# Layer 1's first weights and the kept down weights split behind layer 0's last gate tile, its down products ordered behind its last gate product, and modulation units moved to pairs 12 to 19

## The chip, the cores and the metric

The kernel runs on one core of one Trainium2 chip. A core has five engines with instruction queues of their own: TensorE (PE; the loading of its weights is listed as PEld), VectorE (DVE), ScalarE (ACT), GpSimd (POOL) and SyncE (SP). Transfers are issued from these queues and carried by 16 DMA engines that the core's queues share. The metric is the device time of one execution in microseconds (us). The kernel before takes 1612.67 us, the median of three runs (1612.62 to 1614.48).

## The reference

Two layers of a diffusion backbone work on 512 latent tokens and 256 context tokens of width 1024. Each layer has an attention block and a SwiGLU feed-forward block (FFN) of width 2816. What goes into each block is normalised, scaled and shifted, and what comes out is scaled by a gate. Those factors ("modulation vectors") come from the conditioning vector `c` for the latents, and from `c_ctx` for the context:

```
sh_a, sc_a, g_a, sh_f, sc_f, g_f = split(silu(c) @ mod_w[l] + mod_b[l], 6)
h_lat = h_lat + g_a * mixer(rms_norm(h_lat) * (1 + sc_a) + sh_a)
a     = rms_norm(h_lat) * (1 + sc_f) + sh_f
g, u  = split(a @ w_gate_up[l], 2)
h_lat = h_lat + g_f * ((silu(g) * u) @ w_down[l])
```

The context follows the same path in layer 0, with its own factors; in layer 1 it is only read. The output is the final normalisation of the latents.

## The kernel before, in words

Tokens lie along the free axis, so that a feature tile is 128 rows by 768 columns: `LATS` are the 512 latent columns, `CTXS` the 256 of the context. Products are taken in three matmuls (high by high, high by low, low by high part) of operands that were split into a rounded part and a remainder. ScalarE makes the rounded part (a cast, `S.copy`), VectorE the remainder (a subtraction). `load_w` (lines 313 to 320) loads a weight panel through the buffers "wr" (three of them) and splits it into "wh" and "wl"; `parts` (1328 to 1331) splits a tile into given buffers; `mm3` (322 to 333) issues the three products of a down or output tile.

Instructions on an engine are run in a fixed order. The tile framework works it out in advance, from a simulated timeline of its own, with waits on semaphores for data and for buffers. `behind(ins, *before)` adds an order between instructions on one engine, without a wait.

The FFN (`ffn`, line 1441 and on) works through the 22 pairs of gate and up tiles in chunks, in layer 0 `(0,4), (4,4), (8,4), (12,4), (16,3), (19,3)` as first pair and count. Here they are called chunks 0 to 5. Each pair (`Pair`) uses seven products of 12 matmuls on 384 columns (lines 1342 to 1344) in place of eight, with sums of operands made ahead. In `head`, product "11" goes to the bank z and "21" to x. In `body`, "T2" is added to z, "T3" opens y and "T1" is added to z. In `tail`, "22" is added to z and "T4" to y. Between these, ScalarE copies z (lines 1382, 1389, 1392), VectorE adds x to the copy (1383), ScalarE takes Silu of it (1384), and VectorE reads y (1393) before T4 may be added to it. After T4, lines 1397 to 1402 make the gate tile, which is cast (1329) and split (1330) into the operand of the down products. The tail of a pair is issued behind the head of the next one; the last pair of a chunk has its tail behind the loading of the chunk's first down weight.

After the pairs of a chunk come its down products: for each of eight tiles m, `down0` fetches the residual from DRAM (line 1197, POOL's queue), runs `mm3` on the latent and context columns, adds the result (1193) and stores the tile. In the program's order some of these products stand between the last products of the chunk's pairs. The last chunk of layer 0 uses `final0`: it goes through `output` (1212 on) with all latent tiles first and all context tiles after. Its weights come from `kept_w`, which loads each down weight once and keeps it for the second stream. `kept_w` for m=3, 4 and 5 also loads and splits panels 8, 9 and 0 of layer 1's input weights through "wr". Each latent tile is squared (ACT), and the squares are added by POOL and VectorE (366) to the sum whose product with ones (380) gives the norm of layer 1. The eight latent tiles are then stored in DRAM ("parked", line 1494) from ACT's queue, behind the square root of that norm.

The remaining modulation vectors are made in between. `bg(n)` takes n units from a generator. In this stage a unit (`mod_tile`, the branch for `late`) loads a 512 KB tile of `mod_w` into the single buffer "rope0" from POOL's queue (222) and reduces it on VectorE with the conditioning vector (227, a custom operation and a read of its accumulator). In layer 0's FFN there are 48 such loads; the first 16 tiles are reduced twice in their unit, once for the latents and once for the context, the other 32 once. `ffn` calls `bg(more(j))` after pair j, with

```
BG = ((0, 0, 0, 0, 0), (2, 3), (0, 0), (0, 0))
... lambda j: BG[1][j > 9] if j > 3 else j > 1
```

so that pairs 4 to 9 issue two units each and pairs 10 and on three each, until none is left. After `ffn` "rope0" takes the rotation tables of layer 1.

Of the kernel before, what the change touches and what calls it, by code (L numbers as in the profile page):

```python
# [10 lines left out]
F32R = mybir.dt.float32r  # L11
AF = mybir.ActivationFunctionType
ALU = mybir.AluOpType

P = 128
D = 1024
KT = D // P
# [10 lines left out]
CHUNKS = ((0, 4), (4, 4), (8, 4), (12, 4), (16, 3), (19, 3)), ((0, 3), (3, 3), (6, 4), (10, 4), (14, 4), (18, 4))  # L28
MLA_SCALE = 96.0 ** -0.5
LOWEST = -3.0e38  # L30
LATS = slice(0, NL)
CTXS = slice(NL, NT)
HT = NT // 2
TOK1, TOK2 = slice(0, HT), slice(HT, NT)
# [32 lines left out]
LOWER = 150  # L67
LOE = {(0, 2, 0): None, (0, 2, 1): None, (0, 5, 0): None, (0, 5, 1): 1, (1, 2, 0): None, (1, 2, 1): None, (1, 5, 0): None, (1, 5, 1): None}
PATTERN = ("fbsfbsfbbsfs",) * 3
BG = ((0, 0, 0, 0, 0), (2, 3), (0, 0), (0, 0))  # L70
FIRST = 2000
STEPS = ((2, 3, 4, 4), 5, 3)
HALVES = (slice(0, 256), slice(256, 512))
# [25 lines left out]
def hybrid_kernel(ctx: ExitStack, tc, I, out):  # L99
# [6 lines left out]
    def T(tag, shape, dt=F32):  # L106
        count[0] += 1
        if tag not in SIZES:
            return sb.tile(shape, dt, tag=tag, name=f"{tag}_{count[0]}", bufs=BUFS.get(tag, 1))
        n = int(np.prod(shape[1:]))  # L110
        t = sb.tile([P, SIZES[tag] // (2 if dt == mybir.dt.bfloat16 else 4)], dt, tag=tag, name=f"{tag}_{count[0]}",
                    bufs=BUFS[tag])[: shape[0], :n]
        if len(shape) == 3:
            t = t.rearrange("p (a b) -> p a b", a=shape[1])
        return t

    def B(dt=F32, tag="b"):
        return T(tag, [P, NT], dt)
# [22 lines left out]
    def behind(ins, *before):  # L141

        for x in before:
            tc.add_manual_dep(ins.ins, x.ins.name, mybir.DependencyInfo(mybir.DependencyClass.NoSync,
                              mybir.DependencyReason.DATA), reason="products in one run")
        return ins
# [37 lines left out]
    dense, tile, late, first = [True], [-9], [], {}  # L184
# [128 lines left out]
    def load_w(src, kt, m, eng=None, tag=None, after=()):  # L313

        r = T("wr", [P, kt * m])
        dma(r, src)
        h, lo = (B(F32R, tag)[:, : kt * m] if tag else T(x, [P, kt * m], F32R) for x in ("wh", "wl"))
        behind(S.copy(h, r), *after[:1])  # L318
        behind((G if eng else V).tensor_tensor(lo, r, f(h), op=ALU.subtract), *after[1:])  # L319
        return tuple(x.rearrange("p (k m) -> p k m", k=kt) for x in (h, lo))  # L320

    def mm3(outs, w, mov, first=True, last=True):

        wh, wl = w
        n = len(mov)
        begin = None
        for o, c in outs:
            for k, (mh, ml) in enumerate(mov):
                ins = PE.matmul(o, wh[:, k], mh[:, c], start=first and k == 0, stop=False)  # L329
                begin = begin or ins  # L330
                PE.matmul(o, wh[:, k], ml[:, c], start=False, stop=False)  # L331
                PE.matmul(o, wl[:, k], mh[:, c], start=False, stop=last and k == n - 1)  # L332
        return begin
# [5 lines left out]
    def PQ():  # L339
        return PS("d")  # L340

    outs = [0, None]

    def PO():

# [23 lines left out]
    marks = {}  # L369
# [383 lines left out]
    r = B(tag="nb")  # L753
# [120 lines left out]
    root, diag = first_norm(acc, LATS)  # L874
# [6 lines left out]
    for c in range(4):  # L881
# [5 lines left out]
        sums = []  # L887
# [24 lines left out]
    def beside(gen):  # L912
        side_work.append(gen)
        return gen
# [56 lines left out]
    rope0 = T("rope0", [P, 2, NL])  # L971
# [180 lines left out]
    def mla_jobs():  # L1152
        phase[0], lower[0] = 1, LOWER
        rate[0] = STEPS[1], BG[0][4]
        ready.append(latent_operands(1))
# [22 lines left out]

    H = []
    for k in range(KT):  # L1180
        t = B()
        dma(t, I["xn"][k])
        H.append(t)
    O += [in_rows(o, (B(F32R, "st"), B(F32R, "st"))) for o in OM]

    def add_residual(m, o, l, comp, v, c, dst=None, base=None):
        base = base or H[m]
        if c is TOK2:
            for x, v in pieces(c):
                ins = add_residual(m, o[:, x.start - HT : x.stop - HT], l, comp, v, x, dst, base)  # L1190
            return ins
        g = mod(l, comp, v, m)
        return V.scalar_tensor_tensor((dst or base)[:, c], o, g, base[:, c], op0=ALU.mult, op1=ALU.add)
# [3 lines left out]
        G.dma_start(t[:, c], home[m][:, c])  # L1197
        return t

    ahead, soon = {}, []  # L1200

    def kept_w(src, m):

        if 2 < m < 6:
            soon.append(load_w(I["w_in1"][(8, 9, 0)[m - 3]], KT, P))
        if m in ahead:
            return ahead[m]
        r, t = T("wr", [P, 384]), T("nb", [P, NT], F32R) if m < 2 else B(F32R, "st")
        dma(r, src(m))
        return tuple(x.rearrange("p (k m) -> p k m", k=3) for x in parts(r, t[:, :384], t[:, 384:]))  # L1210

    def output(src, mov, l, comp, streams, norm, units, dst=None, keep=False, base=None, wait=0):

        rest, kept, done = iter(()), [], []
        for i, (c, v) in enumerate(streams):
# [4 lines left out]
            for m in range(KT):  # L1220
# [9 lines left out]
                if c is TOK1:  # L1230
                    G.dma_start(home[m], H[m])
                norm.add(m, c)
# [93 lines left out]
        return Norm(src, use, G if l else None, (0, 4, 1, 5, 2, 6, 3, 7)), ops, sums  # L1326

    def parts(t, h, lo, after=()):
        S.copy(h, t)
        behind(V.tensor_tensor(lo, t, f(h), op=ALU.subtract), *after)  # L1330
        return h, lo

    norm, ops, sums = combined(H, 0, 3, TOK1, TOK2)
    output(lambda m: I["w_out0"][m], O, 0, 2, ((TOK2, 0), (TOK1, 0)), norm, BG[2])


    def product(o, w, x, first=False):

        for k in range(4):
            wh, wl = (y[:, k * P : k * P + P] for y in w)  # L1340
            xh, xl = x[k]
            PE.matmul(o, wh, xh, start=first and k == 0, stop=False, skip_group_check=not first)  # L1342
            PE.matmul(o, wh, xl, start=False, stop=False, skip_group_check=not first)  # L1343
            PE.matmul(o, wl, xh, start=False, stop=k == 3, skip_group_check=not first)  # L1344

    class Pair:

# [47 lines left out]
        def tail(self):  # L1395
            product(self.z, self.s4, self.ops["22"])
            S.activation(self.s[:, self.c2], self.z, AF.Silu)
            product(self.y, self.u2, self.ops["T4"])
            V.tensor_tensor(self.t[:, self.c1], self.y, self.t[:, self.c1], op=ALU.add)
            for c in (self.c2, self.c1) if self.w > NX else (slice(0, 2 * self.w),):  # L1400
                V.tensor_tensor(self.s[:, c], self.s[:, c], self.t[:, c], op=ALU.mult)
                parts(self.s[:, c], *(x[:, c] for x in self.dst))
# [38 lines left out]
    def ffn(l, ops, sums, cs, tags, own, more, down, final):  # L1441

        for ci, (k0, kc) in enumerate(CHUNKS[l]):
            hs, last = [], None
            for j in range(k0, k0 + kc):
                if j == 0:
                    hs.extend(first_pairs(l, ops, cs, tags, own))
                    if l == 0:
                        bg(1)
                    sums()  # L1450
                elif j >= DIRECT[l]:
                    p = Pair(l, j, ops, cs, tags[j - k0], (near_done[3],) if j == DIRECT[l] and l == 0 else ())
                    p.head()
                    if last:
                        last.tail()
                    p.body()
                    hs.append(p.dst)
                    last = p
                bg(more(j))
            src = lambda m: I["w_dn"][l, m, :, k0 * P : (k0 + kc) * P]  # L1460
            ahead.clear()
            ahead[0] = load_w(src(0), kc, P) if l or ci < len(CHUNKS[l]) - 1 else kept_w(src, 0)
            if last:
                last.tail()
            if ci < len(CHUNKS[l]) - 1:
                for m in range(KT):
                    down(m, lambda: ahead.get(m) or load_w(src(m), kc, P), hs)
            else:
                final(src, hs)

    new = []
    norm1, A = modulated(new, 1, 0, G, LATS)
# [9 lines left out]
    def final0(src, hs):  # L1482
        new.extend(B() for _ in range(KT))
        old = [fetched(m, slice(0, NT), "b") for m in range(KT)]
        output(src, hs, 0, 5, STREAMS0, norm1, BG[3], new, kept_w, lambda m, c: old[m], 1)

    ffn(0, ops, sums, (TOK1, TOK2), ("st", "st", "b", "b"), norm.marks[0], lambda j: BG[1][j > 9] if j > 3 else j > 1, down0, final0)
    H = new


    parked = []
    for k in range(KT):
        t = dr.tile([P, NL], F32, name=f"parked{k}")
        behind(S.dma_start(t, H[k][:, LATS]), norm1.marks[0]["root"])
        parked.append(t)
    rope1 = T("rope0", [P, 2, NL])
    dma(rope1, I["rope1"])
# [30 lines left out]
    for t0, n in ((0, 4), (4, 2)):  # L1528
        o = PS("t")
# [40 lines left out]
    H = []  # L1570
    for k in range(KT):
        t = B()
# [3 lines left out]
    norm, ops, sums = combined(H, 1, 3, *HALVES)  # L1576
# [124 lines left out]
```

## Time and profile before

| what | value |
|---|---|
| median of three runs | 1612.67 us (1612.62 to 1614.48) |
| the profiled execution's own time | 1610.99 us |
| its span in the profile | 1609.1 us |
| TensorE busy | 1541.6 us, 96% of the span |
| VectorE busy | 1183.8 us, 74% |
| ScalarE busy | 799.0 us, 50% |
| POOL busy | 298.6 us, 19% |
| layer 0: first product of chunk 3, chunk 4, chunk 5 | 766.40, 860.17, 930.99 us |
| layer 0: the norm's product with ones | 1003.50 us |

A row of the timeline gives the start in us, the duration in us, the engine, the line of the kernel, the operation, output from inputs, sizes and, in brackets, the idle time of the engine just before it with what ended it. Matmuls are pipelined, so their durations overlap: their price is the distance between starts. The page's fifth part lists groups of instructions: busy time and mean duration in ns, then the engine's idle time before them and what ended most of it.

### The profile page before, as it was taken

To read this page: it belongs to the slowest core of one execution; us is meant where nothing else is said; L and a number is where in the kernel's file an instruction comes from. 1 tells how busy PE (TensorE), PEld (TensorE's weight loads), DVE (VectorE), ACT (ScalarE), POOL (GpSimd) and SP (SyncE) were. 2 spreads that over 40 slices of the span, in tenths; PEclk is the share of its full clock that TensorE was granted. 3 is DMA by queue.
4 is the path that set the end of the run, shared out by engine and by line. 5 is a ranking of instruction groups with operands and counts; after the bars stand their busy time and mean duration, and the time that the engine had idled before them with its cause. 6 is when DMAs were issued, how large, how long until landed. Compare 5 with 4: busy or idle time off the path is not lost. (4 is left out here: it accounts for less than half of the span.)

```text
span 1609.1 us, 26559 instructions
## 1 busy us (share of the span) xinstructions
PE 1541.6 (96%) x9990; PEld 1371.1 (85%) x9990; DVE 1183.8 (74%) x2380; ACT 799.0 (50%) x1616; POOL 298.6 (19%) x324
## 2 busy tenths in 40 slices
PE   5989989999999999999999998999999999999997
PEld 3777867776899999998989896877779899899997
DVE  4773878668577678796867686779877688687685
ACT  4452587677365334342423244467756544354453
POOL 0231734230011111102021212384002000000002
PEclk9999999999999999999999998999999999999999
DMA  9634232102453455536456655132005133223322
GB/s 330 226 115 157 70 122 78 40 9 74 165 200 102 152 198 182 203 121 261 170 195 214 235 206 222 66 93 77 2 17 187 38 114 126 86 99 125 87 93 84
DMA packets 76536, 214.91 MB, mean 134 GB/s; under 512 B 10196, under 2 KB 17752, under 8 KB 76408
## 3 DMA queue, kind: packets, MB, share of 16 engines
q1 hardware_dynamic: 57432, 141.67, 26.4%
q0 software_dynamic: 16240, 68.30, 12.1%
q10 hardware_dynamic: 2736, 3.26, 0.6%
q8 instruction: 78, 1.28, 0.3%
q14 instruction: 50, 0.41, 0.1%
HBM read 186.97 MB, written 23.07 MB: 131 GB/s over the span
## 5 line engine op out<-in xcount | busy, mean ns | idle before, releaser
L318 ACT CAST wh<-wr 128x1024 fp32r<-128x1024 f32 (+2 forms) x148 | 114.8, 789 | 203.8 <-DMA wr<-in_w_dn_dram 35.4
L319 DVE TENSOR_TENSOR wl<-wr,wh 128x1024 fp32r<-128x1024 f32 (+2 forms) x145 | 135.1, 938 | 84.6 <-ACT wh L318 80.7
L553 ACT ACTIVATE p<-p,sm 128x512 f32<-128x512 f32 (+3 forms) x144 | 105.0, 730 | 32.4 <-DVE sm L557 30.5
L366 POOL TENSOR_TENSOR p<-p,p 128x256 f32<-128x256 f32 (+1 forms) x33 | 31.7, 960 | 468.5 <-PE psd L332 340.2
L1342 PE MATMUL pss<-b,wh 128*128 128x384 f32 (+1 forms) x344 | 107.0, 312 | 0.6 <-ACT b L355 0.6
L1343 PE MATMUL pss<-b,wh 128*128 128x384 f32 (+1 forms) x344 | 107.2, 312 | 0.1
L227 DVE CUSTOM_DVE_ANT_0 p<-rope,cond 128x1024 bf16<-128x1024 f32 x64 | 77.3, 1224 | 40.8 <-DMA rope<-in_mod_w_dram 40.5
L1344 PE MATMUL pss<-b,wl 128*128 128x384 f32 (+1 forms) x344 | 106.1, 312 | 0.0
L331 PE MATMUL psd<-b,wh 128*128 128x512 f32 (+3 forms) x256 | 88.2, 345 | 0.0
L329 PE MATMUL psd<-b,wh 128*128 128x512 f32 (+3 forms) x216 | 78.4, 363 | 2.9 <-ACT b L493 2.5
L547 PE MATMUL pso<-ph,b 128*64 128x256 f32 (+1 forms) x384 | 77.6, 360 | 2.1 <-DVE ph L492 2.1
L332 PE MATMUL psd<-b,wl 128*128 128x512 f32 (+3 forms) x216 | 77.1, 357 | 0.1
L547 PE MATMUL pso<-pl,b 128*64 128x256 f32 (+1 forms) x384 | 76.9, 359 | 0.2 <-DVE pl L492 0.2
L222 POOL DMA_DIRECT2D rope<-in_mod_w_dram x48 | 25.5, 531 | 244.1 <-DVE mod L227 229.3
L1344 PE MATMUL pst<-b,wl 128*128 128x384 f32 (+1 forms) x224 | 69.9, 312 | 0.0
L1343 PE MATMUL pst<-b,wh 128*128 128x384 f32 (+1 forms) x224 | 69.8, 312 | 0.0
L1342 PE MATMUL pst<-b,wh 128*128 128x384 f32 (+1 forms) x224 | 69.8, 312 | 0.0
L329 PE MATMUL pss<-st,wh 128*128 128x512 f32 (+2 forms) x200 | 68.2, 341 | 1.3 <-ACT st L1144 0.9
L331 PE MATMUL pss<-b,wh 128*128 128x256 f32 (+3 forms) x211 | 68.5, 325 | 0.1
L332 PE MATMUL pss<-st,wl 128*128 128x512 f32 (+2 forms) x200 | 68.0, 341 | 0.1
L1342 PEld LDWEIGHTS pss<-b,wh 128*128 128x128 f32 x344 | 65.2, 190 | 1.1 <-ACT b L355 0.9
L1343 PEld LDWEIGHTS pss<-b,wh 128*128 128x128 f32 x344 | 65.3, 190 | 0.9 <-DVE b L356 0.7
(674 smaller groups left out, 5423.8 us busy)
## 6 DMA issues: line engine op xcount, KB each, us to landing
wr<-in_w_gu_dram SPq DMA_DIRECT2D x88, 512.0 KB, 4.0
rope<-in_mod_w_dram POOLq DMA_DIRECT2D x48, 512.0 KB, 3.8
wr<-in_w_out_dram SPq DMA_DIRECT2D x32, 512.0 KB, 3.7
wr<-in_w_dn_dram SPq DMA_DIRECT2D x64, 256.0 KB, 2.8
p<-home POOLq DMA_DIRECT2D x40, 384.0 KB, 5.6
home<-p POOLq DMA_DIRECT2D x40, 384.0 KB, 5.0
wr<-in_w_in_dram SPq DMA_DIRECT2D x21, 512.0 KB, 3.9
nb<-in_nb_dram SPq DMA_DIRECT2D x16, 384.0 KB, 3.0
```

Of the source, the lines that this page charges most:

```text
L227: V.tensor_tensor_reduce(out=T("p", [P, D], mybir.dt.bfloat16), in0=w, in1=cond[:, v, :], op0=ALU.mult, op1=ALU.add, scale=1.0, scalar=0.0 ...
L318: behind(S.copy(h, r), *after[:1])
L319: behind((G if eng else V).tensor_tensor(lo, r, f(h), op=ALU.subtract), *after[1:])
L329: ins = PE.matmul(o, wh[:, k], mh[:, c], start=first and k == 0, stop=False)
L331: PE.matmul(o, wh[:, k], ml[:, c], start=False, stop=False)
L332: PE.matmul(o, wl[:, k], mh[:, c], start=False, stop=last and k == n - 1)
L366: marks["add"] = (eng or V).tensor_tensor(acc[:, :n], acc[:, :n], t[:, :n], op=ALU.add)
L547: ins = PE.matmul(o[64 * i : 64 * i + 64, c], v(kt), t, start=n == 0, stop=n == len(moving[i]) - 1)
L553: S.activation(p[:, c], p[:, c], AF.Exp, bias=nm, scale=-1.0, accum_out=dn)
L1342: PE.matmul(o, wh, xh, start=first and k == 0, stop=False, skip_group_check=not first)
L1343: PE.matmul(o, wh, xl, start=False, stop=False, skip_group_check=not first)
L1344: PE.matmul(o, wl, xh, start=False, stop=k == 3, skip_group_check=not first)
```

## The change

Five edits.

1. `BG[1]` goes from (2, 3) to (2, 4) and its switch from j > 9 to j > 11. Pairs 4 to 11 issue two units each and pairs 12 to 19 four each; the total of 48 loads stays.
2. `mm3` puts the first product of each output `behind` the list `tail_end`, which holds the last T4 product of the chunk's last pair. It applies to each `mm3` with `first`, in the chunks of both layers; the list is emptied after layer 0's `ffn`, and filled again in layer 1.
3. In the last chunk of layer 0 the kept weights m=0 and 1 are loaded and split ahead of the last tail. From m=2 on their casts and splits are put behind the cast and the split of the last gate tile (`split_behind`, `tails`).
4. Panels 8, 9 and 0 of layer 1's input weights are loaded after kept weights 3, 5 and 7 (before: ahead of 3, 4 and 5), panels 8 and 9 through "rope0" instead of "wr", and are split behind the same tile.
5. The parked stores are issued from POOL's queue, without the order behind the square root.

```diff
-BG = ((0, 0, 0, 0, 0), (2, 3), (0, 0), (0, 0))
+BG = ((0, 0, 0, 0, 0), (2, 4), (0, 0), (0, 0))
...
+        hold = tail_end if first else ()
         for o, c in outs:
             for k, (mh, ml) in enumerate(mov):
                 ins = PE.matmul(o, wh[:, k], mh[:, c], start=first and k == 0, stop=False)
+                if k == 0:
+                    behind(ins, *hold)
...
-    ahead, soon = {}, []
+    ahead, soon, tails = {}, [], []
+
+    def split_behind(r, h, lo):
+
+        behind(S.copy(h, r), *tails[:1])
+        behind(V.tensor_tensor(lo, r, f(h), op=ALU.subtract), *tails[1:])
+        return h, lo
 
     def kept_w(src, m):
 
-        if 2 < m < 6:
-            soon.append(load_w(I["w_in1"][(8, 9, 0)[m - 3]], KT, P))
         if m in ahead:
             return ahead[m]
         r, t = T("wr", [P, 384]), T("nb", [P, NT], F32R) if m < 2 else B(F32R, "st")
         dma(r, src(m))
-        return tuple(x.rearrange("p (k m) -> p k m", k=3) for x in parts(r, t[:, :384], t[:, 384:]))
+        w = split_behind(r, t[:, :384], t[:, 384:])
+        if m in (3, 5, 7):
+            r = T("wr" if m == 7 else "rope0", [P, D])
+            dma(r, I["w_in1"][{3: 8, 5: 9, 7: 0}[m]])
+            soon.append(tuple(x.rearrange("p (k m) -> p k m", k=KT) for x in split_behind(r, *(T(x, [P, D], F32R) for x in ("wh", "wl")))))
+        return tuple(x.rearrange("p (k m) -> p k m", k=3) for x in w)
...
     def parts(t, h, lo, after=()):
-        S.copy(h, t)
-        behind(V.tensor_tensor(lo, t, f(h), op=ALU.subtract), *after)
+        marks["cast"] = S.copy(h, t)
+        marks["split"] = behind(V.tensor_tensor(lo, t, f(h), op=ALU.subtract), *after)
         return h, lo
...
-            product(self.y, self.u2, self.ops["T4"])
+            self.end = product(self.y, self.u2, self.ops["T4"])
...
-            ahead[0] = load_w(src(0), kc, P) if l or ci < len(CHUNKS[l]) - 1 else kept_w(src, 0)
+            tails.clear()
+            if l or ci < len(CHUNKS[l]) - 1:
+                ahead[0] = load_w(src(0), kc, P)
+            else:
+                ahead.update({m: kept_w(src, m) for m in range(2)})
             if last:
                 last.tail()
+                tails[:] = [marks["cast"], marks["split"]]
+                tail_end[:] = [last.end]
...
-    ffn(0, ops, sums, (TOK1, TOK2), ("st", "st", "b", "b"), norm.marks[0], lambda j: BG[1][j > 9] if j > 3 else j > 1, down0, final0)
+    ffn(0, ops, sums, (TOK1, TOK2), ("st", "st", "b", "b"), norm.marks[0], lambda j: BG[1][j > 11] if j > 3 else j > 1, down0, final0)
     H = new
+    tail_end.clear()
...
-        behind(S.dma_start(t, H[k][:, LATS]), norm1.marks[0]["root"])
+        G.dma_start(t, H[k][:, LATS])
```

(`product` in the changed kernel returns its last matmul.)

More of the change, by code (lines that the diff above doesn't have):

```diff
@@ L340, in PQ @@
         return PS("d")
-    outs = [0, None]
+    outs, tail_end = [0, None], []
     def PO():
@@ L1343, in product @@
             PE.matmul(o, wh, xl, start=False, stop=False, skip_group_check=not first)
-            PE.matmul(o, wl, xh, start=False, stop=k == 3, skip_group_check=not first)
+            ins = PE.matmul(o, wl, xh, start=False, stop=k == 3, skip_group_check=not first)
+        return ins
     class Pair:
```

## The prediction

> **What bounds the kernel now.** I read the page's head first, to find the engine that sets the time; then the costliest groups, for the work that the change moves; then the tables by stage, because a share of the whole span says nothing about one chunk; then the timelines of the chunks that the change touches.
>
> ```profile
> span 1609.1 us, 26559 instructions
> PE 1541.6 (96%) x9990; PEld 1371.1 (85%) x9990; DVE 1183.8 (74%) x2380; ACT 799.0 (50%) x1616; POOL 298.6 (19%) x324
> ...
> L227 DVE CUSTOM_DVE_ANT_0 p<-rope,cond 128x1024 bf16<-128x1024 f32 x64 | 77.3, 1224 | 40.8 <-DMA rope<-in_mod_w_dram 40.5
> ...
> L222 POOL DMA_DIRECT2D rope<-in_mod_w_dram x48 | 25.5, 531 | 244.1 <-DVE mod L227 229.3
> ```
>
> TensorE is busy for 96% of the span, so a change wins only by closing one of its few gaps, and loses whatever it opens. The two groups below it are one modulation unit: POOL (L222) loads a 512 KB tile, and VectorE (L227) reduces it. POOL's idle time in front of L222 is 229.3 us, nearly all of it ended by L227: each load waits for the read before it, since "rope0" is a single buffer. VectorE in turn waits for the load, 40.5 us in all. The units are a closed chain.
>
> The two stages that receive the moved units, columns as time range, length, busy time and instructions of PE, PEld, DVE, ACT, POOL, granted clock, DMA share and GB/s:
>
> ```profile
> 772.00:836.00 64.00, 63.10 (x365) 61.56 (x364) 46.47 (x81) 23.30 (x45) 9.01 (x17) 1.00 0.47 158
> 866.00:913.00 47.00, 46.05 (x265) 44.47 (x263) 33.37 (x59) 16.45 (x33) 8.12 (x16) 1.00 0.46 155
> ```
>
> There PE lacks 0.90 of 64 and 0.95 of 47 us, at full clock. The chain is hidden today.
>
> **Price of a unit.** One turn of the chain (start, duration, engine, line), then starts in chunks 3 (pairs 12 to 15) and 4 (pairs 16 to 18):
>
> ```profile
> rope<-in_mod_w_dram POOLq DMA_DIRECT2D x48, 512.0 KB, 3.8
> ```
> ```profile
> 960.85 1.22 DVE L227 CUSTOM_DVE_ANT_0 p<-rope,cond 128x1024 bf16<-128x1024 f32 x1 [0.31 <-DMA rope<-in_mod_w_dram]
> ...
> 962.38 0.53 POOL L222 DMA_DIRECT2D rope<-in_mod_w_dram  x1 [4.86 <-DVE mod L227]
> ...
> 966.14 1.23 DVE L227 CUSTOM_DVE_ANT_0 p<-rope,cond 128x1024 bf16<-128x1024 f32 x1 [3.59 <-DMA rope<-in_mod_w_dram]
> ```
> ```profile
> 772.75 1.22 DVE L227 CUSTOM_DVE_ANT_0 p<-rope,cond 128x1024 bf16<-128x1024 f32 x1
> ...
> 789.45 1.23 DVE L227 CUSTOM_DVE_ANT_0 p<-rope,cond 128x1024 bf16<-128x1024 f32 x1 [1.05 <-DMA rope<-in_mod_w_dram]
> ...
> 794.57 1.23 DVE L227 CUSTOM_DVE_ANT_0 p<-rope,cond 128x1024 bf16<-128x1024 f32 x1 [0.68 <-DMA rope<-in_mod_w_dram]
> ...
> 805.94 1.22 DVE L227 CUSTOM_DVE_ANT_0 p<-rope,cond 128x1024 bf16<-128x1024 f32 x1
> ...
> 822.64 1.23 DVE L227 CUSTOM_DVE_ANT_0 p<-rope,cond 128x1024 bf16<-128x1024 f32 x1 [1.10 <-DMA rope<-in_mod_w_dram]
> ...
> 824.55 0.56 DVE L1393 TENSOR_TENSOR p<-pss,p 128x384 f32<-128x384 f32 x1 [0.20 <-ACT p L1392]
> ...
> 833.42 1.23 DVE L227 CUSTOM_DVE_ANT_0 p<-rope,cond 128x1024 bf16<-128x1024 f32 x1 [2.58 <-DMA rope<-in_mod_w_dram]
> ...
> 834.57 0.55 DVE L1399 TENSOR_TENSOR p<-pss,p 128x384 f32<-128x384 f32 x1
> ...
> 866.76 1.22 DVE L227 CUSTOM_DVE_ANT_0 p<-rope,cond 128x1024 bf16<-128x1024 f32 x1
> ...
> 909.89 1.23 DVE L227 CUSTOM_DVE_ANT_0 p<-rope,cond 128x1024 bf16<-128x1024 f32 x1 [1.82 <-DMA rope<-in_mod_w_dram]
> ```
>
> From read to issue 1.53 us, from issue to the next read 3.76: 5.29 us a unit. In chunk 3, 805.94 is the seventh unit and 833.42 the twelfth: 27.48/5 = 5.50 each. In chunk 4 the ninth comes 43.13 us after the first: 5.39. The shortest interval I found is 5.12 (789.45 to 794.57). VectorE works in a fixed order, so whatever stands behind a unit waits for that chain.
>
> The Trainium skill, "DMA: Bandwidth & Descriptors", section "Anatomy of one DMA — SWDGE (gpsimd) path", gives about 2.0 us plus bytes over 436 GB/s; by it 524,288 bytes would take an estimated 3.2 us, the turn 4.7, and the sum below would come out near 1627. This case's 3.8 us disagrees, and the measurement decides.
>
> PE's work is priced from these rows:
>
> ```profile
> 766.04 0.28 PE L329 MATMUL pst<-b,wh 128*128 128x256 f32 x1
> ...
> 766.40 0.34 PE L1342 MATMUL pss<-b,wh 128*128 128x384 f32 x1
> ...
> 814.38 0.33 PE L1342 MATMUL psd<-st,ph 128*128 128x384 f32 x1
> ...
> 816.46 0.39 PE L329 MATMUL psd<-st,wh 128*128 128x512 f32 x1
> ...
> 860.17 0.34 PE L1342 MATMUL pss<-b,wh 128*128 128x384 f32 x1
> ...
> 930.99 0.34 PE L1342 MATMUL pss<-b,wh 128*128 128x384 f32 x1
> ...
> 970.61 0.45 PE L1342 MATMUL pst<-st,wh 128*128 128x384 f32 x1 [0.57 <-ACT p L1389]
> ...
> 986.55 0.47 PE L329 MATMUL psd<-st,st 128*128 128x512 f32 x1 [1.96 <-DVE p L1399]
> ...
> 991.00 0.79 PE L329 MATMUL pst<-b,nb 128*128 128x512 f32 x1 [2.00 <-ACT b L1329]
> ...
> 997.24 0.39 PE L329 MATMUL pst<-st,st 128*128 128x512 f32 x1
> ...
> 999.28 0.28 PE L329 MATMUL psd<-st,nb 128*128 128x256 f32 x1
> ...
> 1003.50 0.87 PE L380 MATMUL pss<-ones,p 128*128 128x1 f32 x6 [2.98 <-DVE p L366]
> ```
>
> A gate/up product is 12 matmuls: 814.38 to 816.46, 2.08 us; a pair has seven, 14.6 us. Down products: nine of 512 columns take 2.04 (997.24 to 999.28), 0.227 each; three of 256 take 0.36, 0.12 each.
>
> **Term 1, chunk 3: +19.** Four pairs now carry 16 units, not 12. A pair's four units need 4 × 5.4 = 21.6 us, while PE spends 14.6 on it. In the changed program's VectorE order the x read of pair 15 (L1383 of before) stands behind unit 12, its y read (L1393) behind unit 13, its gate tile behind unit 14 and the first down residual behind unit 16. Before, the y read follows unit 10 (822.64, then 824.55) and the gate tile unit 12 (833.42, then 834.57). Unit 12 falls at about 833.4 again, since the chain starts with 772.75 and turns no faster. After it come the unit (1.23), the x read (0.55, as L1399's row), and on ScalarE the Silu, a weight cast and the z copy (three at about 0.5): T1 of pair 15 starts near 836.8. By pure work PE is there 25 products after 766.40, at 818.5, with the earlier gates of pair 14 at 822 to 824. It then idles some 12 us. Before, down products were mixed in at that place (816.46 is one); now each first down product is ordered behind the last T4, so nothing fills. T1 and 22 (4.2) and T4 (behind unit 13, 838.9 plus 1.8, and behind 22) end at 843.7. Eight down tiles of 12 × (0.227 + 0.12) are 33.3 us: the chunk ends near 877.0, not 860.17, +16.8. An idle of that length also brings the lower clock:
>
> ```profile
> 987.00:994.00 7.00, 5.00 (x13) 3.46 (x12) 2.13 (x5) 1.44 (x3) 0.00 (x0) 0.51 1.02 404
> ...
> 1004.00:1008.00 4.00, 4.00 (x22) 4.00 (x23) 1.35 (x3) 0.68 (x2) 0.00 (x0) 0.57 0.61 223
> ```
>
> Behind waits of 2 to 3 us (986.55, 991.00, 1003.50) the clock was 0.51 to 0.57 for 4 to 7 us, which costs half of that, 2 to 3.4. I take +19 (ends +16.8 and +20.2).
>
> The Trainium skill, "TensorE: Matmul & The Clock Gate", section "Part 1: The HAM clock gate", puts the half clock behind an idle window of about 3.4 us. By that the 0.57 us waits below cost no clock and these stalls do; the trace shows it already after 2 us.
>
> **Term 2, chunk 4: +13.4.** With s its first product: the first unit comes at s + 6.59 (866.76 against 860.17), unit 8 at s + 44.3, unit 10 at s + 55.1. Pair 18's x read stands behind unit 8, so T1 starts at s + 47.6, where PE is at s + 37.5 (18 products); its y read is behind unit 10, so T4 runs from s + 56.9 to 59.0. Eight tiles of 9 × 0.347 (25.0) and a 0.3 us switch end at s + 84.2, against 70.82 (930.99 less 860.17). Ends: +10 if the first units start 3 us earlier, +16.8 with a full dip of the clock.
>
> **Term 3, chunk 5 with the last output: -7.3.** Today 930.99 to 1003.50, 72.51 us, holds the waits 0.57, 1.96, 2.00 and 2.98 and the half clock. Changed: 252 matmuls × 0.1735 (43.7, plus 0.8 waits), 72 × 0.227 (16.4), nine of 256 (1.1), and 3.2 for residual, square and sums behind the last product, as between 1000.09 and 1003.50 in these rows:
>
> ```profile
> 1000.09 0.74 DVE L1193 SCALAR_TENSOR_TENSOR b<-pst,mod,b 128x512 f32<-128x512 f32 x1
> ...
> 1002.75 0.69 DVE L366 TENSOR_TENSOR p<-p,p 128x512 f32<-128x512 f32 x1
> ```
>
> That is 65.2. The kept weights m=0 and 1 are split before the gate tile, the rest behind it, so the waits on L1399 and L1329 go. The four units left there and the loads of panels 8, 9, 0 issue earlier and lie beside products. Two things are uncovered: panels 8 and 9 pass through "rope0" one after the other on SP's queue, with weight m=7 behind them (0 to +3.8, a landing); and the eight parked stores now stand in POOL's queue between its sums, seven of 0.53 us ahead of the third sum (0 to +3.7). I count both at 0, with under 1 us to spare. So the gain lies between 7.3 and nothing.
>
> **Term 4, held down products elsewhere: +4.6.** In chunks 0, 1, 2 and the five last tails of layer 1 nothing fills the wait between T2 and T1 for the z copy any more; it is 0.57 where the trace shows it unfilled (970.61). Eight times 0.57; ends 0 and +4.6, nearer the upper, since it is the same pair of products. Emptying pairs 4 to 11 of no unit, and giving chunk 2 two fewer, is worth nothing: those pairs hide them.
>
> **Sum.** 19 + 13.4 - 7.3 + 4.6 = +29.7. The profiled execution's own time is 1610.99, 1.7 below the median of 1612.67: 1640.7, forecast 1640.
>
> **Rivals.** A, the other side: the chain stays hidden. Unit 12 plus 3.4 would have to come before 818.5, so the turn may be no longer than (818.5 - 3.4 - 772.75)/11 = 3.85 us, below the 5.12 seen and hardly above the landing alone. For it: PE lost only 0.90 us in this stage. Then terms 1 and 2 vanish: 1611.0 - 7.3 + 2.3 (half of term 4) = 1606, faster. B, the same with all of term 4 and 3 us of term 3 lost: 1611.3, no change. C, milder: the turn is 4.7 us, as if issues overlapped reads; unit 12 falls 8 us earlier, chunk 4's tenth unit 6: 1640 - 7 - 6 = 1627. D, dearer: both stalls with the full dip, and term 3 given back by parked stores or panel loads: 1640.7 + 1.2 + 3.4 + 5 = 1650. Against D: the margins, though thin; for it, the DMA share of 1.02 in 987 to 994.
>
> **How the numbers follow.** Forecast 0.64, A 0.05, B 0.03, C 0.11, D 0.17. The range 1622 to 1652 takes in the forecast, C and most of D and leaves out A and B. Changes under 0.2% (3.2 us) can't be told from none here: faster 0.05 (A), same 0.03 (B), slower 0.92.
>
> **What would show it.** Right: L227 in chunks 3 and 4 back to back at 5.3 to 5.5 us; PE idle of 8 to 12 us ended by VectorE or ScalarE shortly ahead of the first down product of each; clock below 1 behind it; chunk 5 some 7 us shorter, without waits on L1399 and L1329; 0.57 us waits at the other tails. Wrong: a turn under 4.5 us, or x and y reads of pairs 15 and 18 that do not stand behind their units.

## The result and the profile after

The changed kernel takes 1642.64 us (median of five runs, 1641.59 to 1642.75), the kernel before, run beside it, 1613.51 us: a ratio of 1.0183, with a 95% interval of 1.0170 to 1.0196. It is slower by 29 us, where 1640 us was forecast. The profiled spans differ by 1639.8 - 1609.1 = 30.7 us, and that is what the parts below divide up.

The head of the changed kernel's page, and its row for a unit's reduction:

```profile
span 1639.8 us, 26564 instructions
...
PE 1551.4 (95%) x9990; PEld 1379.8 (84%) x9990; DVE 1187.1 (72%) x2380; ACT 799.7 (49%) x1616; POOL 303.3 (18%) x332
...
L227 DVE CUSTOM_DVE_ANT_0 p<-rope,cond 128x1024 bf16<-128x1024 f32 x64 | 77.2, 1223 | 46.4 <-DMA rope<-in_mod_w_dram 46.2
```

Nothing of this names the cause: TensorE's busy time grew by 9.8 us for the same 9990 matmuls, the other engines' by 4.7 us or less, and VectorE's wait for tiles grew from 40.5 to 46.2 us only. The stages tell it. The tables of windows, with the columns of the prediction, cut at the first products of chunks 3, 4 and 5 and at the norm's product; the kernel before:

```profile
766.40:860.17 93.77, 92.71 (x530) 87.73 (x529) 68.34 (x118) 32.79 (x60) 14.95 (x28) 1.00 0.58 202
860.17:930.99 70.82, 69.82 (x398) 65.90 (x397) 51.02 (x90) 23.95 (x46) 13.35 (x25) 1.00 0.61 217
930.99:1003.50 72.51, 64.75 (x336) 59.47 (x334) 55.34 (x94) 32.58 (x57) 13.22 (x20) 0.95 0.59 209
```

and the changed kernel:

```profile
766.44:877.15 110.71, 97.04 (x530) 90.60 (x529) 73.39 (x125) 32.81 (x60) 17.09 (x32) 0.95 0.53 183
877.15:962.33 85.18, 75.04 (x398) 69.86 (x397) 51.53 (x90) 23.54 (x44) 14.44 (x27) 0.90 0.54 190
962.33:1030.75 68.42, 62.13 (x336) 57.88 (x334) 54.24 (x88) 31.93 (x58) 15.22 (x24) 0.99 0.60 216
```

At the start of chunk 3 the two stand 0.04 us apart, which hides two differences: the changed kernel began layer 0's FFN 1.66 us sooner (513.25 against 514.91), in a stretch that the change doesn't touch, and its chunks 0 to 2 are longer by 0.47, 0.93 and 0.30, 1.70 in all. Chunk 3 is longer by 16.94 us, chunk 4 by 14.36, chunk 5 shorter by 4.09; what follows the norm's product is longer by 609.05 - 605.60 = 3.45. The same matmuls are spread over more time: in chunk 3 PE lacks 13.7 us, in place of 1.1.

The stall itself, in VectorE's timeline of the changed kernel (L1396 is the read of x, L1406 that of y):

```profile
771.34 1.22 DVE L227 CUSTOM_DVE_ANT_0 p<-rope,cond 128x1024 bf16<-128x1024 f32 x1
...
826.28 1.23 DVE L227 CUSTOM_DVE_ANT_0 p<-rope,cond 128x1024 bf16<-128x1024 f32 x1 [1.33 <-DMA rope<-in_mod_w_dram]
...
831.51 1.23 DVE L227 CUSTOM_DVE_ANT_0 p<-rope,cond 128x1024 bf16<-128x1024 f32 x1 [3.99 <-DMA rope<-in_mod_w_dram]
...
832.66 0.56 DVE L1396 TENSOR_TENSOR p<-pst,p 128x384 f32<-128x384 f32 x1
...
836.86 1.22 DVE L227 CUSTOM_DVE_ANT_0 p<-rope,cond 128x1024 bf16<-128x1024 f32 x1 [3.65 <-DMA rope<-in_mod_w_dram]
...
839.37 0.56 DVE L1406 TENSOR_TENSOR p<-pss,p 128x384 f32<-128x384 f32 x1 [0.68 <-ACT p L1405]
...
853.69 1.23 DVE L227 CUSTOM_DVE_ANT_0 p<-rope,cond 128x1024 bf16<-128x1024 f32 x1 [1.73 <-DMA rope<-in_mod_w_dram]
```

in ScalarE's (L1397 is Silu, L1402 the copy of z):

```profile
833.25 0.52 ACT L1397 ACTIVATE p<-p 128x384 f32<-128x384 f32 x1 [8.51 <-DVE p L1396]
...
834.18 0.47 ACT L1402 COPY p<-pss 128x384 f32<-128x384 f32 x1
```

and in TensorE's, with the ends of chunks 4 and 5:

```profile
813.69 0.44 PE L1354 MATMUL pst<-st,wh 128*128 128x384 f32 x1 [1.43 <-ACT p L1402]
816.66 0.44 PE L1354 MATMUL pst<-b,wh 128*128 128x384 f32 x1 [0.62 <-ACT p L1405]
...
824.79 0.69 PE L1354 MATMUL pss<-st,wh 128*128 128x384 f32 x1 [3.69 <-ACT p L1395]
...
834.71 0.69 PE L1354 MATMUL pss<-st,wh 128*128 128x384 f32 x1 [6.01 <-ACT p L1402]
...
839.39 0.44 PE L1354 MATMUL pss<-b,wh 128*128 128x384 f32 x1 [0.62 <-ACT p L1405]
...
843.66 0.39 PE L330 MATMUL psd<-st,wh 128*128 128x512 f32 x1
...
924.93 0.69 PE L1354 MATMUL pst<-st,wh 128*128 128x384 f32 x1 [5.36 <-ACT p L1402]
935.00 0.45 PE L1354 MATMUL psd<-st,ph 128*128 128x384 f32 x1 [1.03 <-DVE p L1406]
937.22 0.39 PE L330 MATMUL pss<-st,wh 128*128 128x512 f32 x1
...
968.89 0.44 PE L1356 MATMUL pst<-st,wl 128*128 128x384 f32 x1 [1.74 <-DVE wl L1342]
986.84 0.44 PE L1356 MATMUL pst<-b,wl 128*128 128x384 f32 x1 [0.61 <-DVE wl L1342]
1030.75 1.86 PE L383 MATMUL pss<-ones,p 128*128 128x1 f32 x8 [3.94 <-DVE p L369]
```

Read it backwards: T1 of pair 15 starts at 834.71 after 6.01 us of idleness that the copy of z ends; the copy stands behind Silu, which waited 8.51 us for the read of x; and the read of x follows unit 12 at once, for whose tile VectorE had waited 3.99 us. The sixteen units of the chunk take (853.69 - 771.34)/15 = 5.49 us each. The clock around the two stalls:

```profile
820.00:835.00 15.00, 5.30 (x20) 4.67 (x19) 7.30 (x13) 2.81 (x6) 1.59 (x3) 0.77 0.32 94
835.00:843.00 8.00, 7.38 (x33) 7.01 (x33) 2.75 (x5) 1.49 (x3) 0.53 (x1) 0.78 0.45 152
843.00:850.00 7.00, 7.00 (x40) 6.12 (x39) 5.24 (x10) 1.03 (x2) 0.58 (x2) 1.00 0.33 115
...
916.00:937.00 21.00, 13.90 (x47) 12.39 (x48) 7.82 (x15) 3.23 (x8) 2.12 (x4) 0.59 0.32 97
937.00:945.00 8.00, 8.00 (x47) 7.03 (x46) 4.29 (x7) 0.52 (x2) 4.24 (x8) 1.00 0.60 216
```

### The profile page after: what moved, and what is told of

Read it like the earlier page. It is cut to its first block, busy times and chain, and to the rows that moved or that the text cites. A ratio compares the mean times of both kernels' runs of the same rounds, so it can differ in the third digit from the quotient of the medians.

```text
span 1639.8 us, 26564 instructions
## 1 busy us (share of the span) xinstructions
PE 1551.4 (95%) x9990; PEld 1379.8 (84%) x9990; DVE 1187.1 (72%) x2380; ACT 799.7 (49%) x1616; POOL 303.3 (18%) x332
## 5 line engine op out<-in xcount | busy, mean ns | idle before, releaser
L319 DVE TENSOR_TENSOR wl<-wr,wh 128x1024 fp32r<-128x1024 f32 (+2 forms) x142 | 131.6, 932 | 63.1 <-ACT wh L318 62.3
L227 DVE CUSTOM_DVE_ANT_0 p<-rope,cond 128x1024 bf16<-128x1024 f32 x64 | 77.2, 1223 | 46.4 <-DMA rope<-in_mod_w_dram 46.2
L1354 PE MATMUL pst<-b,wh 128*128 128x384 f32 (+1 forms) x224 | 72.0, 321 | 3.0 <-ACT p L1405 3.0
L1355 PE MATMUL pst<-b,wh 128*128 128x384 f32 (+1 forms) x224 | 71.3, 319 | 0.0
```

The lines of the kernel that those rows point to most:

```text
L227: V.tensor_tensor_reduce(out=T("p", [P, D], mybir.dt.bfloat16), in0=w, in1=cond[:, v, :], op0=ALU.mult, op1=ALU.add, scale=1.0, scalar=0.0 ...
```

## The experiments

The theory: the units are a closed chain of 5.3 to 5.5 us a turn, and four of them last longer than a pair's 14.6 us. Rival 1: the order put on the down products is what costs, since it takes from TensorE the work that filled its waits. Rival 2: the traffic around the last chunk costs (panels that queue for one buffer, parked stores between POOL's sums). The lengths of the stages in the profiled executions, in us; "rest" runs from the norm's product to the end:

| kernel | chunk 1 | chunk 2 | chunk 3 | chunk 4 | chunk 5 | rest |
|---|---|---|---|---|---|---|
| before | 91.70 | 92.33 | 93.77 | 70.82 | 72.51 | 605.60 |
| changed | 92.63 | 92.63 | 110.71 | 85.18 | 68.42 | 609.05 |
| units back | 92.66 | 93.89 | 97.41 | 72.92 | 72.91 | 611.21 |
| units alone | 91.83 | 91.73 | 111.10 | 85.24 | 68.85 | 606.18 |
| hold alone | 92.63 | 93.85 | 95.91 | 74.39 | 69.50 | 609.74 |
| units back, last chunk held | 92.09 | 93.03 | 94.45 | 71.09 | 73.59 | 613.32 |
| half units | 92.63 | 92.65 | 93.93 | 70.87 | 69.28 | 609.83 |
| two buffers | 93.10 | 93.08 | 96.32 | 69.72 | 69.21 | 610.64 |
| its control | 92.65 | 92.67 | 113.01 | 84.55 | 66.95 | 610.58 |
| parked stores back | 92.64 | 92.63 | 111.15 | 86.50 | 66.48 | 610.79 |

**The units alone, in the kernel before.**

```diff
-BG = ((0, 0, 0, 0, 0), (2, 3), (0, 0), (0, 0))
+BG = ((0, 0, 0, 0, 0), (2, 4), (0, 0), (0, 0))
...
-BG[1][j > 9]
+BG[1][j > 11]
```

> The kernel before with the units of the change alone (two a pair to pair 11, four from 12 to 19). Theory: T1 and T4 of pairs 15 and 18 wait for the same units, but 36 and 24 down matmuls stand between the last gate products here and run in those waits, about 6 and 4 us: chunk 3 some +11, chunk 4 some +9, last chunk about -3: 1625 to 1632 us. Rival 1 (holding is the cost): 1610 to 1614. Rival 2: 1610 to 1614.

Measured 1640.81 us, 1.0182 of before (1.0150 to 1.0214): the whole loss. Rivals 1 and 2 are gone as its main cause, since neither of their edits is in this kernel. But the theory's number was missed too: I had the down products fill 6 and 4 us of the waits. They did run earlier, and chunks 3 and 4 still take 111.10 and 85.24. One of TensorE's rows and two of VectorE's from this kernel show why:

```profile
832.75 0.80 PE L329 MATMUL pss<-st,wh 128*128 128x512 f32 x1 [6.62 <-ACT wh L318]
```
```profile
846.30 1.23 DVE L227 CUSTOM_DVE_ANT_0 p<-rope,cond 128x1024 bf16<-128x1024 f32 x1 [1.76 <-DMA rope<-in_mod_w_dram]
847.45 0.55 DVE L1399 TENSOR_TENSOR p<-pss,p 128x384 f32<-128x384 f32 x1
```

The cast of the next down weight stands on ScalarE behind the Silu that waits for unit 12, so the products that should have filled the wait had no weight. And here the gate tile's operation L1399 stands behind unit 15, a unit later than in the changed kernel. Where the units come later than the work that stands behind them, they set when the chunk ends, and other work for TensorE didn't help here.

**The order of the down products alone, in the kernel before.**

```diff
+        hold = tail_end if first else ()
...
+                if k == 0:
+                    behind(ins, *hold)
...
+                tail_end[:] = [last.end]
```

> The kernel before with the down products ordered behind the last T4, and nothing else. Theory: an unfilled wait of about 0.6 us for a z copy at each tail (+1.5 to +5 in all) and up to 2 us in chunk 3 where the y read stands behind unit 10: 1613 to 1619 us. Rival 1 (holding is the cost): 1630 or more. Rival 2: as before, 1613.

1620.08 us, 1.0049 (1.0034 to 1.0064): 6.6 us, a little over the range. Chunks 2, 3 and 4 lose 1.5, 2.1 and 3.6, since T1 waits there 0.95 to 2.8 us for a z copy with nothing to fill it (the row is chunk 4's); chunk 1 loses 0.9 and the rest behind the norm 4.1; chunk 5 gains 3.0. So holding has a price of its own, a quarter of the loss, when the units lie as before. In the changed kernel, where the chain sets the ends of chunks 3 and 4 anyway, it adds nothing there: 110.71 and 85.18 with it, 111.10 and 85.24 without.

```profile
903.90 0.44 PE L1345 MATMUL pst<-st,wh 128*128 128x384 f32 x1 [2.82 <-ACT p L1393]
```

**The units back, all else as changed.**

```diff
-BG = ((0, 0, 0, 0, 0), (2, 4), (0, 0), (0, 0))
+BG = ((0, 0, 0, 0, 0), (2, 3), (0, 0), (0, 0))
...
-BG[1][j > 11]
+BG[1][j > 9]
```

> The changed kernel with the units spread as before (two a pair in pairs 4 to 9, three from pair 10), all else as changed. Theory (the chain of units, 5.3 to 5.5 us a turn, outruns the pairs): chunk 3 needs its y read behind unit 10 again, the idles of 6 to 12 us in chunks 3 and 4 go, what is left is the held down products and a last chunk with nine units: 1612 to 1618 us. Rival 1 (the held down products are the cost, the units only sit there): still 1635 to 1643. Rival 2 (panel loads through the single buffer and parked stores on POOL cost it): still above 1630, with the loss in the last chunk of layer 0.

1627.43 us, 1.0097 (1.0070 to 1.0124). The stalls go, as the theory has it, but 14 us remain, and the range is missed by 9. By the table chunks 2 to 4 are 7.3 us longer, as with the held down products alone (7.2), and most of the rest is lost around the last chunk: with nine units in it, it is no shorter than before (72.91), the wait for the norm in it is 7.57 us in place of 2.98, and the stage behind it is 5.6 us longer. So part of what rival 2 names is real, once the units are late.

**The units back, the down products held in the last chunk alone.** Beside the edit above:

```diff
-                tail_end[:] = [last.end]
+                tail_end[:] = [last.end] if not l and ci == len(CHUNKS[l]) - 1 else []
```

> The changed kernel with the units spread as before and the down products held in the last chunk of layer 0 alone; kept weights, panels and parked stores as changed. Theory: chunks 0 to 4 and layer 1 as in the kernel before, the last chunk shorter than its 72.5 us by 0 to 4, less than with four units since it has nine: 1608 to 1613 us. Rival 1: about 1613. Rival 2 (panels and parked stores cost): 1618 or more, lost between 930 and 1010 us.

1618.21 us, 1.0032 (1.0019 to 1.0044), above the theory's range. Chunks 1 to 4 come back to within 0.7 us; chunk 5 is 1.1 us longer than before, where 0 to 4 less was expected, and the stages behind it 7.7. Rival 2 has the side right here, though most of it lies later than it said: 0.84 up to the next projection, 2.25 in it (waits of 1.00 and 0.31 for VectorE's normalised tiles, L419, are part of that), 2.6 in the attention, 2.0 in the FFN and the final norm, for which I have no cause shown. The loss in the last chunk can be seen. In POOL's timeline of this kernel, and TensorE's wait for the norm:

```profile
996.63 0.54 POOL L1514 DMA_DIRECT2D parked<-b  x1 [1.50 <-DVE b L1196]
997.23 4.77 POOL L369 TENSOR_TENSOR p<-p,p 128x512 f32<-128x512 f32 x3
```
```profile
1003.58 1.87 PE L383 MATMUL pss<-ones,p 128*128 128x1 f32 x8 [7.57 <-DVE p L369]
```

All eight parked stores stand ahead of POOL's three sums, and the last waits for the last tile's residual. The sums then run one after the other, 4.77 us, though ScalarE had five of the eight squares ready by 992.4. The wait for the norm is 4.6 us longer than before, more than the 1.1 that the chunk lost: by this estimate it would be some 3.5 shorter without it, inside the theory's 0 to 4. In the changed kernel the order was kinder, with the stores between the sums.

**The parked stores back on ACT's queue, in the changed kernel.**

```diff
-        G.dma_start(t, H[k][:, LATS])
+        behind(S.dma_start(t, H[k][:, LATS]), norm1.marks[0]["root"])
```

> The changed kernel with the parked stores back on ACT's queue behind the square root. Theory: the stores were counted at nothing; the sums on POOL lose 0.5 us issues ahead of them, so the wait for the norm shrinks by 0 to 2 us: 1639 to 1643 us. Rival 1: no change. Rival 2 (panels and parked stores cost the time): 10 us or more faster, 1632 or less.

1640.75 us, 1.0155 (1.0120 to 1.0190), against the changed kernel's 1.0183 (1.0170 to 1.0196). The two ratios overlap, so a gain isn't shown in the time. In the profile the wait for the norm is 2.35 in place of 3.94 us, and chunk 5 takes 66.48 in place of 68.42, but what follows is 1.74 longer in that execution:

```profile
1032.71 1.70 PE L383 MATMUL pss<-ones,p 128*128 128x1 f32 x8 [2.35 <-DVE p L369]
```

Why the stores lengthen this wait shows in POOL's and VectorE's rows of the changed kernel, and in the same sum of VectorE's with the stores on ACT's queue:

```profile
1026.09 0.54 POOL L1514 DMA_DIRECT2D parked<-b  x1 [2.63 <-DVE b L1196]
1026.64 1.39 POOL L369 TENSOR_TENSOR p<-p,p 128x512 f32<-128x512 f32 x1
```
```profile
1026.84 1.74 DVE L369 TENSOR_TENSOR p<-p,p 128x512 f32<-128x512 f32 x1
```
```profile
1029.87 0.68 DVE L369 TENSOR_TENSOR p<-p,p 128x512 f32<-128x512 f32 x1
```

POOL's third sum stands behind the seventh store, which waits for its tile, and so runs beside VectorE's sum, with the last residual behind it. That sum takes 1.74 us, and 0.68 where POOL's sums are over by 1025. A split beside POOL's second sum took 1.74 in place of 1.21. The 1.06 and 0.53 make up the 1.59 by which the wait shrinks.

**Half the work in a unit, in the changed kernel.**

```diff
-            G.dma_start(w, I["mod_w"][at])
+            G.dma_start(w[:, :512], I["mod_w"][at, :, :512])
...
-... in0=w, in1=cond[:, v, :], ...
+... in0=w[:, :512], in1=cond[:, v, :512], ...
```

> The changed kernel with units of half the work: each loads and reduces 512 of the 1024 columns of its tile, so half of each late modulation product is left out. Theory: the turn falls from 5.4 to about 3.6 to 4.2 us (0.6 less for the reduction, 0.6 to 1.2 less for 256 KB less to land), so four units take about a pair's 14.6 us and the idles of chunks 3 and 4 go, apart from the held down products: chunk 3 from 110.7 to 95 to 99 us, chunk 4 from 85.2 to 71 to 75, in all 1612 to 1622 us. Rival 1 (held down products): chunks as long as in the changed kernel, 1640. Rival 2 (panel loads and parked stores): likewise about 1640.

1613.09 us, 0.9998 of before (0.9983 to 1.0012). This kernel leaves out half of each late modulation product, so it is a probe and no candidate. With a shorter turn (and 0.54 us less for VectorE in each reduction) the whole loss is gone. From this kernel's table of transfers, VectorE's timeline (the first and the last of the sixteen units of chunk 3) and the windows of chunks 3 and 4:

```profile
rope<-in_mod_w_dram POOLq DMA_DIRECT2D x48, 256.0 KB, 2.9
```
```profile
771.19 0.68 DVE L227 CUSTOM_DVE_ANT_0 p<-rope,cond 128x512 bf16<-128x512 f32 x1
...
831.81 0.69 DVE L227 CUSTOM_DVE_ANT_0 p<-rope,cond 128x512 bf16<-128x512 f32 x1 [0.56 <-DMA rope<-in_mod_w_dram]
```
```profile
766.29:860.22 93.93, 92.35 (x531) 87.72 (x529) 65.27 (x125) 32.90 (x60) 17.14 (x32) 1.00 0.53 178
860.22:931.09 70.87, 69.40 (x399) 65.73 (x398) 46.00 (x93) 23.17 (x44) 14.46 (x27) 1.00 0.51 182
```

The turn is (831.81 - 771.19)/15 = 4.04 us, four of them 16.2, and chunks 3 and 4 are as long as before to 0.2 us. The prediction's bound for a hidden chain was 3.85 us, counted so that TensorE never waits for unit 12; at 4.04 T1 of the last pairs waits 0.95 and 0.85 us for its z copy, and the chunks don't grow.

**Two buffers for the tiles, and its control.**

```diff
-BUFS = dict(b=24, ..., p=8, ...)
+BUFS = dict(rope0=2, b=24, ..., p=7, ...)
```

> The changed kernel with two buffers for the units' tiles (and seven buffers p in place of eight, to make room). Theory: a load no longer waits for the read before it, so the turn falls below 4 us, and chunks 3 and 4 come back to 95 to 100 and 71 to 76 us, unless the missing buffer p costs: 1612 to 1625 us, and 15 to 30 below its control. Rival 1: as its control, no stall less. Rival 2: less time in the last chunk alone, since the panels no longer queue for one buffer; chunks 3 and 4 as long as before.

> The control for two buffers: the changed kernel with seven buffers p in place of eight and one buffer for the tiles. Theory: units and pairs as in the changed kernel, 1640 to 1655 us, depending on what the missing buffer costs. The rivals expect the same.

1619.13 us against the control's 1647.92 (1.0039, 1.0026 to 1.0052, against 1.0209, 1.0183 to 1.0235): 28.8 us less with whole tiles and the same transfers, by taking away the wait of the load for the read. VectorE's units of chunk 3 and the windows of chunks 3 and 4 with two buffers:

```profile
777.41 1.22 DVE L227 CUSTOM_DVE_ANT_0 p<-rope,cond 128x1024 bf16<-128x1024 f32 x1
...
826.79 1.23 DVE L227 CUSTOM_DVE_ANT_0 p<-rope,cond 128x1024 bf16<-128x1024 f32 x1 [0.41 <-DMA rope<-in_mod_w_dram]
```
```profile
772.51:868.83 96.32, 93.78 (x531) 89.27 (x530) 71.85 (x125) 32.13 (x60) 17.08 (x32) 0.98 0.65 215
868.83:938.55 69.72, 69.10 (x399) 65.75 (x398) 52.80 (x94) 25.17 (x47) 14.42 (x27) 1.00 0.69 233
```

The turn falls to (826.79 - 777.41)/15 = 3.29 us. The control takes 1.0209 of before and the changed kernel 1.0183, with intervals that overlap, so a price of the missing buffer p isn't shown. Two buffers make no better kernel, but they settle the cause.

**Four versions that might beat both.** First, the kernel before with the down products held in the last chunk alone (the order as above, with the condition `if not l and ci == len(CHUNKS[l]) - 1`):

> The kernel before with the down products held behind the last T4 in the last chunk of layer 0 alone. With all chunks held the last one took 69.5 us in place of 72.5, and chunks 2 to 4 lost 7; this keeps the first without the second. Theory (holding pays only where the weights and residuals behind the gate tile are what is late, and costs where a z copy or a y read is): 1609 to 1612 us. Rival (the 69.5 came from the order of the other chunks): 1613 to 1615.

1610.95 us, 0.9988 (0.9974 to 1.0003), as expected. Chunk 5 is 69.30 us, so the gain of chunk 5 with all chunks held did come from its own order; whether the kernel is faster the interval leaves open. Second, the same with units put into the down products:

```diff
                 for m in range(KT):
                     down(m, lambda: ahead.get(m) or load_w(src(m), kc, P), hs)
+                    if not l and ci and m in (2, 5):
+                        bg(1)
```

> As the kernel before with the last chunk held, and with two units behind the down products m=2 and m=5 of chunks 1 to 4, so that the pairs need fewer and only one unit is left for the last chunk. Theory (a unit costs nothing where the products beside it last longer than its 5.4 us turn): chunks 1 to 4 within 1 us of before, the last chunk 3 to 5 us shorter: 1606 to 1611 us. Rival (a unit ahead of a residual holds up the down products as it holds up the gate tile): chunks 1 to 4 longer by 2 to 5 us each, 1615 or more.

1612.00 us, 0.9987 (0.9972 to 1.0002). Third, these units alone in the kernel before:

> The kernel before with the two units behind the down products m=2 and m=5 of chunks 1 to 4, and no order on the down products. Theory: chunks 1 to 4 as before, in the last chunk the waits on the gate tile (1.96) and on the cast (2.00) shrink since no unit stands ahead of them: 1608 to 1612 us. Rival: as for the run before this one, 1615 or more.

1613.58 us, 0.9997 (0.9985 to 1.0009). Fourth, the changed kernel's last chunk with parked stores on ACT's queue, the down products held there alone, `BG` as before and units in the down products:

> The changed kernel's last chunk (two kept weights ahead of the gate tile, the others and the panels behind it, panels 8 and 9 through the units' buffer, down products held there alone, parked stores back on ACT) with the units spread as in the two runs before: one is left for the last chunk. Theory: the last chunk 4 to 6 us shorter than before, the others as before: 1606 to 1611 us. Rival 2 (panels in one buffer cost): 1613 or more, lost behind the norm of layer 1 where the panels are first used.

1611.65 us, 0.9985 (0.9972 to 0.9998). In the second to the fourth, chunk 5 takes 66.94 to 67.30 us, some 5 less than before, but chunks 1 to 4 are longer by 5.8 to 7.5 in sum (chunk 2 by 3.1 to 3.5 in each). So a unit among the down products isn't free, though it costs less than the rival of the second run had it: 1.4 to 1.9 us a chunk on average. Two places show in all three traces. Among the down products of chunk 1 TensorE waits 0.69 to 0.84 us for a residual addition that stands behind a unit's two reductions, as the rival says. In the first pair of chunk 2 it waits for split weights, 0.74 and then 1.22 us in the second version; there VectorE and ScalarE had waited for the weights' load, and why that came late is not shown. The second, third and fourth miss their ranges by 0.7 to 1.6 us. Nothing here is faster by as much as 0.2%; only the fourth's interval lies wholly below 1.

## Why the prediction was right, step by step

**The price of a unit.** 5.3 to 5.5 us were read from the kernel before, 5.49 came in chunk 3 and (921.84 - 882.75)/7 = 5.58 from the first to the eighth unit of chunk 4. The two runs that shortened the turn took the loss away. An estimate of 4.7 us a turn from the Trainium skill, "DMA: Bandwidth & Descriptors", section "Anatomy of one DMA — SWDGE (gpsimd) path", isn't borne out. Half a tile landed in 2.9 us where its formula gives 2.6, a whole one in 3.8 where it gives 3.2.

**Term 1, chunk 3: +19 predicted, +16.94 measured.** By the stall alone it was +16.8; the rest was for the lower clock behind it. The first down product was put at 843.7 and came at 843.66, the end at 877.0 and 877.15, but two misses cancel in that, so it is luck. The stall was shorter: the chain started 1.4 us sooner than before (771.34), unit 12 came at 831.51 and not at 833.4, and T1 at 834.71 and not at 836.8. The lower clock took the gain back, at another place than predicted. From T1 to 22 pair 14 took 816.66 - 813.69 = 2.97 us at full clock (1.00 over 805 to 820), pair 15 took 839.39 - 834.71 = 4.68, some 1.7 more. TensorE was last there, since VectorE's y read, clear of unit 13 and a split, waited 0.68 us for the copy of z behind T1. The clock was 0.77 and 0.78 up to 843 and back at 1.00 with the first down products, so those 33 us paid nothing, where the prediction had put its 2.2. The idleness was predicted in one piece of 12 us, and came as 3.69 ahead of T2, 6.01 ahead of T1 and smaller ones, because on ScalarE the first copy of z already waits behind pair 14's gate tile, and that behind unit 10.

**Term 2, chunk 4: +13.4 predicted, +14.36 measured.** From its first product, T1 was put at 47.6 us and came at 47.8, T4 at 56.9 and 57.9, the first down product at 59.0 and 60.1 (937.22). The extra microsecond is the turn: the first unit came 1.0 us sooner than predicted, and nine turns of 5.6 in place of 5.39 cost 2.0. The clock was 0.59 through 916 to 937 and 1.00 behind. Here the dip cost nothing, since T4 still waited 1.03 us for the y read behind unit 10.

**Term 3, chunk 5: -7.3 predicted, -4.09 measured.** This is the term that was mis-sized. The waits on the gate tile and the weight cast did go. But two waits on split weights came (1.74 at 968.89 and 0.61 at 986.84, in place of 0.8), 1.55 more, and the wait for the norm grew from 2.98 to 3.94, 0.74 more than the 3.2 that I had counted for everything behind the last product (the two times that the 3.2 was taken from are 3.4 apart). For the other 0.9 no cause is shown. The parked stores were priced at nothing with "under 1 us to spare"; by the rows above they lengthen the wait by 1.59 us. Their risk was named and given the wrong value: what matters is not 0.53 us an issue, but that a store waits for its tile and all that stands behind it in POOL's queue waits too, here until it runs beside VectorE's last sums.

**Term 4: +4.6 predicted, about 5 measured.** In layer 0, chunks 0 to 2 are 1.70 us longer, where three waits of 0.57 are 1.71. In layer 1, the FFN from the first product of its first `Pair` to its last down product takes 303.64 us against 300.25, 3.39 more, where five waits of 0.57 are 2.85. This is no chance of one execution: in the profiles of the seven kernels that hold all down products it takes 302.4 to 303.6, in the other seven 300.1 to 301.5. The waits are there, 0.62 at the tails of chunks 1 and 2, and in layer 1 at five tails, 2.5 us in all, from the first to the last

```profile
1353.84 0.39 PE L1354 MATMUL pst<-b,wh 128*128 128x256 f32 x1 [0.46 <-ACT p L1405]
...
1602.05 0.39 PE L1354 MATMUL pst<-b,wh 128*128 128x256 f32 x1 [0.62 <-ACT p L1405]
```

They stand one product later than predicted: 22 waits for the copy of z behind T1, and not T1 for the one behind T2. Behind its last down product the changed kernel is 1.7 us shorter, and between the norm's product and layer 1's FFN 1.7 longer, so that +3.45 is left for all that follows the norm. Of the second 1.7, 1.04 come ahead of the next projection and go with the clock: in the 6 us behind the norm's product it is 0.53, and 0.72 in the kernel before. For 0.66 in the attention I have no cause shown.

**The sum.** +29.7 predicted, +30.7 by the spans. The difference of 1.0 is made of -2.1 in term 1, +1.0 in term 2, +3.2 in term 3, +0.5 in term 4 (1.70 + 3.45 in place of 4.6) and -1.7 from the stretch ahead of layer 0's FFN that the change doesn't touch. The mechanism was right; that the sum came so near is in part luck.

**The rivals.** A and B, the hidden chain, needed a turn of 3.85 us or less; the half units show that the threshold was about there. C, 4.7 us, did not occur. D, the full dip of the clock with the last chunk's gain lost, occurred in part: about 1.7 us of the dip in chunk 3, none in chunk 4, and 3.2 of the 7.3.

## What to carry to other kernels

Background work in a single buffer is a clock of its own: measure one turn from read to read, and compare turns per stage with the stage's length before moving any. With an engine's fixed order, everything behind such a step runs at that clock; work elsewhere fills the wait only if its own operands don't stand in the same line. A store put into a queue that also computes holds up what is behind it until its data exist; price it by that wait, not by its issue.

## What the runs showed of the hardware that was not expected

The lower clock behind a stall cost little here, and only where TensorE was the last to be ready. In chunk 4, T1 and 22 ran in the dip (0.59 over 916 to 937), but T4 waited 1.03 us for VectorE even so, and the dip cost nothing. In chunk 3, nothing else held T1 and 22 up, and it cost some 1.7 us. In both the clock was 1.00 in the first 7 to 8 us of the long run of down products behind (843 to 850, 937 to 945). That the products in a dip can be held up by the next wait had no place in my pricing from the kernel before.

An addition on VectorE took 1.74 us in place of 0.68 while POOL made one of its sums, and a split 1.74 in place of 1.21.

Two loads of 512 KB in flight at once brought the turn from 5.49 to 3.29 us, while the median landing stayed about the same, 3.9 us against 3.8.
